# The MLP's second multiplication: three of eight weight units in seven block products, groups of 1024 columns over all PSUM banks

## The chip, the cores and the metric

The kernel runs on one core of a Trainium2 chip (trn2). Its time is the device time of one execution in microseconds (us). The kernel before takes 1953.93 us, the median of 3 runs (1953.6 to 1954.25). TensorE (PE in the profile) multiplies, VectorE (DVE) and ScalarE (ACT) prepare operands and take results away, GpSimd (POOL) does small work, and SyncE (SP) issues most of the DMAs.

## The reference

One decoder layer on 256 tokens of width 2048: a combined attention and retention layer, a cross attention, and an MLP. The change touches only the MLP and the norm at its end:

```python
D_FF = 4 * D_MODEL                                   # 8192
nm = rmsnorm(h, mlp_norm_w)
h = h + jnp.square(jax.nn.relu(nm @ w_up)) @ w_down  # (256, 2048) @ (2048, 8192), then (256, 8192) @ (8192, 2048)
...
return rmsnorm(h, final_norm_w)
```

All arrays are float32, and so is the result.

## The kernel before

TensorE multiplies in a one-pass format that holds fewer bits than float32. So each operand is split into a high part `hi` and a rest `lo` (`split`, L161 to L163): ScalarE copies the source into `hi` (L162), then VectorE computes `lo` = source - `hi` (L163), one instruction each for 128 partitions by 1024 elements. A product then takes three matmuls: hi by hi, hi by lo, lo by hi (`mul`, L158).

Weights come as a stream. `chunk` (L189) takes one of three `raw` buffers of 1 MB, issues one DMA for it on SP's queue (L195), and splits it into two pairs of `hi` and `lo` tiles; there are four buffers of each. A `raw` buffer is free for the next DMA when VectorE has read it last, and a `hi` or `lo` buffer when TensorE has.

The MLP (`mlp`) works in two halves of 4096 hidden columns. In the first part of a half, called *up* here, eight `wgroup` calls multiply by `w_up`, with the weights as TensorE's stationary operand and matmuls of 256 columns. After each group `up_evac` takes the PSUM result through ReLU on ScalarE (L1052), a product on VectorE (L1053) and a split into `hh` and `hl`, which hold hidden columns on the partitions. In the second part, *down*, four `xgroup` calls multiply by 512 columns of `w_down` each, over 4096 rows. There the hidden tiles are stationary and the weights move through, 512 columns per matmul, for two tiles of 128 tokens (i = 0 and 1). `down_evac` adds the PSUM result, times `r2`, to the residual `hres` (L1066). In the last half it also takes the squares (L1073), the product with the final gain (L1076) and, at the very end, the scale by the final norm and the output DMAs (L1090, L1091).

The order of the instructions on each engine is made when the kernel is built, by a scheduler that goes by the dependencies and its own costs; the engine then runs its list in that order. PSUM has eight banks of 512 float32 per partition: two tiles of two banks (`mm`), three of one (`ps`), one of one (`po`). SBUF tiles of 1024 float32 (`big`) come from a pool of 30.

Of the kernel before, what the change touches and what calls it, by code (L numbers as in the profile page):

```python
# [17 lines left out]
P = 128  # L18
# [47 lines left out]
class Kern:  # L66
# [104 lines left out]
    def rsqrt(self, out, v, s):  # L171
# [213 lines left out]
    def retention(self):  # L385
# [242 lines left out]
    def keys(self):  # L628
# [255 lines left out]
    def merge(self):  # L884
# [58 lines left out]
    def cross(self):  # L943
# [70 lines left out]
        for h in range(2):  # L1014
# [8 lines left out]
                                        rows=512) for j in range(4)]))  # L1023

    def mlp(self):
        nc, a = self.nc, self.a
        V, A, G, PE = nc.vector, nc.scalar, nc.gpsimd, nc.tensor
        hres = [None] * 4
        s8, r2 = self.keep("hs8", [2, 4]), self.keep("r2", [2])

        # the residual with tokens on the partitions, and its mean square
        def back(j, i):
            if i == 0:
                hres[j] = self.big("hres", F32, (2, 512))
# [3 lines left out]
            V.tensor_copy(hres[j][:, i, :], pt)  # L1038
# [9 lines left out]

        def up_evac(hh, hl):
# [9 lines left out]
        f8, ft = self.keep("fs", [2, 4]), self.keep("ft", [2])  # L1059
        fw, outs = [], []  # L1060

        # hidden = relu(u)^2 with u not yet divided by the rms: 1 / (mean square) at the end
        def down_evac(f, j):
            def evac(i, ps):
                o = hres[j][:, i, :]
                V.scalar_tensor_tensor(o, ps, r2[:, i:i + 1], o, op0=ALU.mult, op1=ALU.add)  # L1066
                if f == 0:
                    return
                if not fw:
                    fw.append(self.raw())  # L1070
                    nc.sync.dma_start(fw[0], a["final_norm_w"].partition_broadcast(P))
                junk = self.w2("junk")
                A.activation(junk, o, AF.Square, accum_out=f8[:, i, j:j + 1])  # L1073
                if i == 0:
                    outs.append(self.big("out", F32, (2, 512)))
                V.tensor_tensor(outs[j][:, i, :], o, fw[0][:, j * 512:(j + 1) * 512], op=ALU.mult)  # L1076
                v = ft[:, i:i + 1]
                if j == 2:
                    V.tensor_reduce(v, f8[:, i, 0:3], axis=AX.X, op=ALU.add)
                    V.tensor_scalar(v, v, 1.0 / D, EPS, op0=ALU.mult, op1=ALU.add)  # L1080
                if j < 3:
# [47 lines left out]
```

## Time and profile before

| | |
|---|---|
| median of 3 runs | 1953.93 us |
| the profiled execution: span of its instructions | 1951.9 us |
| the runs' median less this span | 2.0 us |
| TensorE busy | 1933.5 us (99%) |
| VectorE busy | 1145.7 us (59%) |
| ScalarE busy | 937.3 us (48%) |

The page gives the span, from the first to the last instruction; what lies around it, some 2 us, is in the time of a run and not in the span. The busy share of TensorE is of pipelined matmuls, whose records overlap, so the pace is read from their starts. The MLP takes the span from about 1238 us on: up, down, up, down, with the borders at 1402.7, 1569 and 1764.8 us.

### The profile page before, as it was taken

How to read it: one execution, taken by the hardware profiler on the slowest of the kernel's cores; microseconds unless marked ns; L12 is line 12 of the kernel's file. 1: busy time of each engine (PE TensorE's matmuls, PEld its weight loads, DVE VectorE, ACT ScalarE, POOL GpSimd, SP SyncE). 2: the span in 40 equal slices, each digit the busy share in tenths (PEclk: the TensorE clock that was granted, in tenths of full speed). 3: DMA queues.
4: the chain of work that ended last, by engine and by line, in shares of the span. 5: the costliest groups of instructions: out<-in, count | busy, mean ns of one | idle time of the engine just before them, and what ended most of it. 6: DMA issues, size and time to landing. Idle time of an engine off the chain costs nothing.

```text
span 1951.9 us, 28137 instructions
## 1 busy us (share of the span) xinstructions
PE 1933.5 (99%) x11606; PEld 1714.9 (88%) x11606; DVE 1145.7 (59%) x1327; ACT 937.3 (48%) x1214; POOL 85.3 (4%) x101
## 2 busy tenths in 40 slices
PE   8999999999999999999999999999999999999998
PEld 6888889888899999888889999999988899998886
DVE  6554577555756666886556756555544445554454
ACT  6444444454555555766445545544433344444442
POOL 1100021000000000321000000000000000000000
PEclk9999999999999999999999999999999999999999
DMA  7555544677876775434566654565655555655554
GB/s 269 210 174 192 186 172 175 229 249 245 274 248 244 248 254 176 137 112 140 184 208 232 208 173 154 172 191 177 193 184 184 193 189 179 189 178 194 188 179 151
DMA packets 190017, 382.29 MB, mean 196 GB/s; under 512 B 10576, under 2 KB 18768, under 8 KB 189760
## 3 DMA queue, kind: packets, MB, share of 16 engines
q1 hardware_dynamic: 185872, 375.01, 57.2%
q10 hardware_dynamic: 3216, 3.15, 0.5%
q0 software_dynamic: 800, 2.33, 0.4%
q8 instruction: 91, 1.49, 0.3%
q14 instruction: 38, 0.31, 0.0%
HBM read 374.17 MB, written 6.29 MB: 195 GB/s over the span
## 4 chain that ended last, share of the span: by engine, by line
PE 97%; DVE 1%; ACT 0%; issue 0%; DMA 0%; POOLq 0%; POOL 0%; DVEq 0%
PE x L158 52%; PE w L158 36%; PE acc L158 3%; PE o L158 1%; PE s L158 1%; PE ro L158 1%; PE pT L816 1%; DMA anw<-in_attn_norm_w_dram 0%; DVE lo L163 0%; PE tr L287 0%; PE rs L158 0%; ACT hi L162 0%; DVE bl L163 0%; PE xo L158 0%; PE g L158 0%
## 5 line engine op out<-in xcount | busy, mean ns | idle before, releaser
L163 DVE TENSOR_TENSOR lo<-raw,hi 128x1024 fp32r<-128x1024 f32 x688 | 848.6, 1240 | 702.8 <-ACT hi L162 688.1
L162 ACT ACTIVATE hi<-raw 128x1024 fp32r<-128x1024 f32 x688 | 724.1, 1059 | 913.2 <-PE x L158 526.0
L158 PE MATMUL w<-nh,hi 128*128 128x256 f32 x1088 | 308.2, 283 | 0.0
L158 PE MATMUL w<-nh,lo 128*128 128x256 f32 x1088 | 307.5, 283 | 0.0
L158 PE MATMUL w<-nl,hi 128*128 128x256 f32 x1088 | 306.9, 282 | 0.0
L158 PE MATMUL x<-hi,xh 128*128 128x512 f32 x704 | 282.5, 401 | 2.2 <-ACT hi L162 2.2
L158 PE MATMUL x<-hi,xl 128*128 128x512 f32 x704 | 278.0, 395 | 0.0
L158 PE MATMUL x<-lo,xh 128*128 128x512 f32 x704 | 277.2, 394 | 0.0
L158 PEld LDWEIGHTS w<-nl,hi 128*128 128x128 f32 x1088 | 207.1, 190 | 0.0
L158 PEld LDWEIGHTS w<-nh,hi 128*128 128x128 f32 x1088 | 207.1, 190 | 0.0
L158 PEld LDWEIGHTS w<-nh,lo 128*128 128x128 f32 x1088 | 206.8, 190 | 0.0
L158 PE MATMUL x<-hi,hl 128*128 128x512 f32 x512 | 202.7, 396 | 0.0
L158 PE MATMUL x<-hi,hh 128*128 128x512 f32 x512 | 202.3, 395 | 0.0
L158 PE MATMUL x<-lo,hh 128*128 128x512 f32 x512 | 201.0, 393 | 0.0
L158 PEld LDWEIGHTS x<-lo,xh 128*128 128x128 f32 x704 | 133.1, 189 | 30.9 <-DVE lo L163 0.8
L158 PEld LDWEIGHTS x<-hi,xh 128*128 128x128 f32 x704 | 132.8, 189 | 30.1 <-ACT hi L162 2.6
L158 PEld LDWEIGHTS x<-hi,xl 128*128 128x128 f32 x704 | 132.8, 189 | 26.5
L158 PE MATMUL w<-xh,hi 128*128 128x256 f32 x512 | 145.3, 284 | 0.0
L158 PE MATMUL w<-xh,lo 128*128 128x256 f32 x512 | 144.2, 282 | 0.0
L158 PE MATMUL w<-xl,hi 128*128 128x256 f32 x512 | 144.1, 281 | 0.0
L158 PEld LDWEIGHTS x<-lo,hh 128*128 128x128 f32 x512 | 96.6, 189 | 22.7
L158 PEld LDWEIGHTS x<-hi,hh 128*128 128x128 f32 x512 | 96.2, 188 | 23.1
(257 smaller groups left out, 2572.9 us busy)
## 6 DMA issues: line engine op xcount, KB each, us to landing
raw<-in_w_in_dram SPq DMA_DIRECT2D x119, 1024.0 KB, 4.9
raw<-in_w_up_dram SPq DMA_DIRECT2D x64, 1024.0 KB, 5.3
raw<-in_w_down_dram SPq DMA_DIRECT2D x64, 1024.0 KB, 5.1
raw<-in_cmp_w_k_dram SPq DMA_DIRECT2D x16, 1024.0 KB, 4.9
raw<-in_w_b_dram SPq DMA_DIRECT2D x16, 1024.0 KB, 5.2
raw<-in_cmp_w_v_dram SPq DMA_DIRECT2D x16, 1024.0 KB, 5.0
raw<-in_w_a_dram SPq DMA_DIRECT2D x16, 1024.0 KB, 5.1
raw<-in_w_out_dram SPq DMA_DIRECT2D x16, 1024.0 KB, 5.1
```

The lines of the kernel that those rows point to most:

```text
L158: self.pin(self.nc.tensor.matmul(out, l, r, start=start, stop=stop, skip_group_check=True))
L162: self.pin(self.nc.scalar.activation(hi, src, AF.Copy))
L163: self.pin(self.nc.vector.tensor_tensor(lo, src, hi.bitcast(F32), op=ALU.subtract))
L816: PE.transpose(pt[:, r * P:(r + 1) * P], sms[r // 2][:, r % 2, c:c + P], self.ident)
```

## The change

The down part is computed in *units* of 256 rows by 1024 columns of `w_down`: a 2 by 2 grid of blocks, each 128 rows by 512 columns, against a 2 by 2 grid of hidden blocks (two row tiles by two token tiles). A plain unit (P) does the eight block products as before, 24 matmuls. A unit of kind S does seven (Strassen's scheme, in Winograd's form), 21 matmuls, with sums of blocks as operands. The kinds of the eight units of a group are "SPPSPSPP".

- The hidden columns now go in four passes (p = 0 to 3) of 2048 in place of two halves of 4096: four `wgroup` calls, then two groups (c = 0 and 1) of 1024 output columns over the eight units of the pass.
- For each S unit, `up_evac` also makes four sums of hidden blocks (`unit_sums`: four VectorE instructions of 128x128, one split of 512).
- For each S unit, `seven` makes four combinations of weight blocks on VectorE (`f1` of 1024, two of 512 into `f2`), and splits them and the four plain blocks: splits of 512, 1024, 1024 and 1024, where a plain unit has two of 1024.
- A group holds all eight PSUM banks: four for results that go straight to the output (`xa`, `xb`), four for the products m1, m5, m6, m7. These four are summed after the last S unit (`down_combine`).
- At the end, the product with the final gain is done in place in `hres`, in tiles of 1024.

```diff
+    def unit_sums(self, y, u, wide):
...
+        s1, s2, s3, s4 = (s[:, k * P:(k + 1) * P] for k in range(4))
+        V.tensor_tensor(s1, a21, a22, op=ALU.add)
+        V.tensor_tensor(s2, s1, a11, op=ALU.subtract)
+        V.tensor_tensor(s3, a21, a11, op=ALU.subtract)
+        V.tensor_tensor(s4, a12, s2, op=ALU.subtract)
+        self.split(sh, sl, s)
...
+    def ugroup(self, w, r0, c0, kinds, ah, al, sums, combine, evac, tail=1):
...
+        ab, cd = self.mmt("xa"), self.mmt("xb")
+        bank[2], bank[3] = ab[:, :512], ab[:, 512:]
+        bank[4], bank[8] = cd[:, :512], cd[:, 512:]
...
+        def plain(us):
...
+                    self.split(h, l, raw[:, k * 1024:(k + 1) * 1024])
...
+            for i in range(2):
+                for j in range(2):
+                    for u in us:
+                        for k in range(2):
+                            product((2, 3, 4, 8)[2 * i + j], act(u, k, i), B[u, k, j], u == n - 1 and k == 1)
+                if us[-1] == n - 1:
+                    evac(i, (ab, cd)[i])
+                yield
+
+        def seven(u):
+            raw = load(u)
+            q = raw.rearrange("p (q n) -> p q n", q=4)
+            f1, f2 = self.big("t1", F32, (2, 512)), self.big("t2", F32, (2, 512))
+            V.tensor_tensor(f1, q[:, 1:2, :].to_broadcast([P, 2, 512]), q[:, 0::3, :], op=ALU.subtract)
+            V.tensor_tensor(f2[:, 0, :], q[:, 3, :], f1[:, 0, :], op=ALU.subtract)
+            V.tensor_tensor(f2[:, 1, :], q[:, 2, :], f2[:, 0, :], op=ALU.subtract)
+            dh, dl = hilo()
+            self.split(dh[:, :512], dl[:, :512], q[:, 0, :])
+            (h1, t1), (h2, t2) = [[self.big(n, F32R, (2, 512)) for n in ("th", "tl")] for _ in range(2)]
+            self.split(h1, t1, f1)
+            self.split(h2, t2, f2)
+            bh, bl = hilo()
+            self.split(bh, bl, raw[:, 1024:])
...
+            for k, m in enumerate((1, 5, 7, 6, 4, 2, 3)):
+                product(m, x[m], b[m], u == last_s and m in (1, 5, 6, 7))
...
     def mlp(self):
...
+        KINDS = "SPPSPSPP"
+        NP = 4
...
+        def down_combine(c):
+            def combine(bank):
...
+                A.activation(x[:, :512], bank[1], AF.Copy)
+                V.tensor_tensor(u2, bank[6], x[:, :512], op=ALU.add)
+                V.tensor_tensor(y[:, :512], bank[7], u2, op=ALU.add)
+                V.tensor_tensor(x[:, 512:], bank[5], u2, op=ALU.add)
+                V.tensor_tensor(y[:, 512:], bank[5], y[:, :512], op=ALU.add)
+                for i, t in enumerate((x, y)):
+                    o = hres[i, c]
+                    V.scalar_tensor_tensor(o, t, r2[:, i:i + 1], o, op0=ALU.mult, op1=ALU.add)
...
-        for f in range(2):
-            hh, hl = [], []
-            self.run(self.seq(*[self.wgroup(a["w_up"][0], f * 4096 + 512 * j, self.h2h, self.h2l, up_evac(hh, hl))
-                                for j in range(8)]))
-            self.run(self.seq(*[self.xgroup(a["w_down"][0], 512 * j, hh, hl, down_evac(f, j), r0=f * 4096, rows=4096,
-                                            last=(f == 1 and j == 3)) for j in range(4)]))
+        for p in range(NP):
+            hh, hl, sums = [], [], {}
+            self.run(self.seq(*[self.wgroup(a["w_up"][0], p * 2048 + 512 * j, self.h2h, self.h2l,
+                                            up_evac(hh, hl, sums)) for j in range(4)]))
+            self.run(self.seq(*[self.ugroup(a["w_down"][0], p * 2048, 1024 * c, KINDS, hh, hl, sums,
+                                            down_combine(c), down_evac(p, c), tail=2 if (p, c) == (NP - 1, 1) else 1)
+                                for c in range(2)]))
```

Below, U0 to U7 are the units of the first group (c = 0) of a pass and V0 to V7 those of the second; U0, U3, U5, V0, V3 and V5 are of kind S.

First place: VectorE's list where up ends and down begins. Before, around the product with ReLU of the last up group (L1053):

```order
L163 TENSOR_TENSOR lo_12830<-raw_12827,hi_12829 128x1024
L163 TENSOR_TENSOR lo_12834<-raw_12827,hi_12833 128x1024
L1053 TENSOR_TENSOR relu_12785<-relu_12785,w_12552 128x1024
L163 TENSOR_TENSOR lo_12864<-raw_12861,hi_12863 128x1024
L163 TENSOR_TENSOR hl_12789<-relu_12785,hh_12788 128x1024
L163 TENSOR_TENSOR lo_12868<-raw_12861,hi_12867 128x1024
L163 TENSOR_TENSOR lo_12898<-raw_12895,hi_12897 128x1024
```

Behind that product stand one weight split, the split of the hidden tile (`hl`) and more weight splits. Now, at the same place of pass p = 0 (raw_11860 is U0, raw_11908 U1, raw_11942 U2, raw_11976 U3; L1103 is `f1`, L1104 and L1105 the two halves of `f2`, `tl` the rests of their splits):

```order
L163 TENSOR_TENSOR lo_11915<-raw_11908,hi_11914 128x1024
L1169 TENSOR_TENSOR relu_11851<-relu_11851,w_11618 128x1024
L163 TENSOR_TENSOR lo_11945<-raw_11942,hi_11944 128x1024
L163 TENSOR_TENSOR hl_11855<-relu_11851,hh_11854 128x1024
L1103 TENSOR_TENSOR t_1823_11862<-raw_11860 128x1024
L1104 TENSOR_TENSOR t_1824_11863<-raw_11860,t_1823_11862 128x512
L1105 TENSOR_TENSOR t_1824_11863<-raw_11860,t_1824_11863 128x512
L163 TENSOR_TENSOR tl_11872<-t_1823_11862,th_11871 128x1024
L163 TENSOR_TENSOR tl_11874<-t_1824_11863,th_11873 128x1024
L1103 TENSOR_TENSOR t_1848_11978<-raw_11976 128x1024
L1104 TENSOR_TENSOR t_1849_11979<-raw_11976,t_1848_11978 128x512
L1105 TENSOR_TENSOR t_1849_11979<-raw_11976,t_1849_11979 128x512
```

The combinations of U0 stand behind the product with ReLU (now L1169) and behind `hl`; those of U3 follow, ahead of the second split of U2. The four passes have the same order here.

Second place: TensorE's list at the same border. Before, the last two matmuls of up and the first of down (`hi_12795` and `lo_12796` are the weights, `hh` and `hl` the hidden tiles):

```order
L158 MATMUL w_12552<-nl_10788,hi_12733 128x256
L158 MATMUL w_12552<-nh_10787,lo_12734 128x256
L158 MATMUL x_12792<-hi_12795,hh_11071 128x512
L158 MATMUL x_12792<-hi_12795,hl_11072 128x512
L158 MATMUL x_12792<-lo_12796,hh_11071 128x512
L158 MATMUL x_12792<-hi_12795,hh_11071 128x512
```

Now, in pass p = 0, where m_1833, m_1836, m_1835 and m_1834 are the banks of m1, m5, m7 and m6:

```order
L158 MATMUL w_11618<-nh_10787,lo_11800 128x256
L158 MATMUL m_1833_11883<-hi_11867,hh_11071 128x512
L158 MATMUL m_1833_11883<-hi_11867,hl_11072 128x512
L158 MATMUL m_1833_11883<-lo_11868,hh_11071 128x512
L158 MATMUL m_1836_11886<-th_11871,sh_11076 128x512
L158 MATMUL m_1836_11886<-th_11871,sl_11077 128x512
L158 MATMUL m_1835_11885<-th_11871,sh_11076 128x512
L158 MATMUL m_1836_11886<-tl_11872,sh_11076 128x512
L158 MATMUL m_1835_11885<-th_11871,sl_11077 128x512
L158 MATMUL m_1835_11885<-tl_11872,sh_11076 128x512
L158 MATMUL m_1834_11884<-th_11873,sh_11076 128x512
```

Three matmuls of U0 (m1) follow the up part; from the fourth on TensorE's list needs `th_11871`, the high part of `f1`.

Third place: VectorE's list in the last down part. Before, where its second column group has ended (the evacuations of L1066, then the products with the gain):

```order
L163 TENSOR_TENSOR lo_16416<-raw_16413,hi_16415 128x1024
L1066 SCALAR_TENSOR_TENSOR hres_10993<-x_16096,r_10798,hres_10993 128x512 x2
L1076 TENSOR_TENSOR out_16372<-hres_10993,raw_16086 128x512 x2
L163 TENSOR_TENSOR lo_16420<-raw_16413,hi_16419 128x1024
L163 TENSOR_TENSOR lo_16450<-raw_16447,hi_16449 128x1024
```

Now, in pass p = 3 between its groups c = 0 and c = 1 (raw_17070 is V0, raw_17118 V1, raw_17152 V2; `xa` and `xb` are c = 0's results):

```order
L1200 SCALAR_TENSOR_TENSOR hres_10894<-xa_16736,r_10798,hres_10894 128x1024
L1209 TENSOR_TENSOR hres_10894<-hres_10894,fw_17043 128x1024
L1212 TENSOR_SCALAR ft<-fs 128x1
L1200 SCALAR_TENSOR_TENSOR hres_10949<-xb_16737,r_10798,hres_10949 128x1024
L163 TENSOR_TENSOR lo_17121<-raw_17118,hi_17120 128x1024
L1103 TENSOR_TENSOR t_2608_17072<-raw_17070 128x1024
L1209 TENSOR_TENSOR hres_10949<-hres_10949,fw_17043 128x1024
L1212 TENSOR_SCALAR ft<-fs 128x1
L1104 TENSOR_TENSOR t_2609_17073<-raw_17070,t_2608_17072 128x512
L163 TENSOR_TENSOR lo_17125<-raw_17118,hi_17124 128x1024
L1105 TENSOR_TENSOR t_2609_17073<-raw_17070,t_2609_17073 128x512
L163 TENSOR_TENSOR tl_17082<-t_2608_17072,th_17081 128x1024
```

The combinations of V0 stand behind both evacuations of c = 0 here; in the passes p = 0 to 2 `f1` of the second group's first unit stands ahead of them.

## Rows read from the trace of the kernel before

**Rows 1.** The page, engines: busy us (share), instructions.
```profile
PE 1933.5 (99%) x11606; PEld 1714.9 (88%) x11606; DVE 1145.7 (59%) x1327; ACT 937.3 (48%) x1214; POOL 85.3 (4%) x101
```
**Rows 2.** The page, chain that ended last: shares of the span.
```profile
PE 97%; DVE 1%; ACT 0%; issue 0%; DMA 0%; POOLq 0%; POOL 0%; DVEq 0%
```
**Rows 3.** The chain in order of time, MLP: start us, us, work, count.
```profile
1402.86 178.38 PE x L158 x768
1581.24 183.60 PE w L158 x1536
```
**Rows 4.** Windows, first up and down: us, busy of PE, PEld, DVE, ACT, POOL, PEclk, DMA.
```profile
1238.00:1402.00 164.00, 164.00 (x1377) 164.00 (x1376) 88.96 (x79) 75.66 (x81) 0.00 (x0) 1.00 0.57 182
1403.00:1569.00 166.00, 166.00 (x716) 134.41 (x715) 79.21 (x68) 65.28 (x62) 0.00 (x0) 1.00 0.56 187
```
**Rows 5.** Timeline, TensorE, first matmul of down: start us, us, instruction.
```profile
1402.69 0.40 PE L158 MATMUL x<-hi,hh 128*128 128x512 f32 x1
```
**Rows 6.** Timeline, ScalarE, same border: in brackets, idle before and releaser.
```profile
1402.78 1.06 ACT L162 ACTIVATE hi<-raw 128x1024 fp32r<-128x1024 f32 x1 [1.82 <-PE w L158]
1403.74 1.01 ACT L1052 ACTIVATE relu<-w 128x1024 f32<-128x1024 f32 x1
1405.47 1.06 ACT L162 ACTIVATE hi<-raw 128x1024 fp32r<-128x1024 f32 x1 [0.72 <-PE x L158]
1406.44 1.04 ACT L162 ACTIVATE hh<-relu 128x1024 fp32r<-128x1024 f32 x1
```
**Rows 7.** Timeline, VectorE, same border.
```profile
1403.87 1.23 DVE L163 TENSOR_TENSOR lo<-raw,hi 128x1024 fp32r<-128x1024 f32 x1 [1.66 <-ACT hi L162]
1405.01 1.21 DVE L1053 TENSOR_TENSOR relu<-relu,w 128x1024 f32<-128x1024 f32 x1
1406.57 1.23 DVE L163 TENSOR_TENSOR lo<-raw,hi 128x1024 fp32r<-128x1024 f32 x1 [0.34 <-ACT hi L162]
1407.71 1.22 DVE L163 TENSOR_TENSOR hl<-relu,hh 128x1024 fp32r<-128x1024 f32 x1
```
**Rows 8.** Groups by line and shape, VectorE, then ScalarE: busy us, mean ns, idle.
```profile
L163 DVE TENSOR_TENSOR pl<-pT,ph 128x512 fp32r<-128x512 f32 x24 | 16.4, 682 | 0.4
...
L1066 DVE SCALAR_TENSOR_TENSOR hres<-x,r,hres 128x512 f32<-128x512 f32 x16 | 11.4, 747 | 10.3 <-PE x L158 10.3
...
L163 DVE TENSOR_TENSOR kcat<-ky,kcat 128x128 fp32r<-128x128 f32 x16 | 3.4, 284 | 0.0
...
L162 ACT ACTIVATE blk<-blkf 128x512 fp32r<-128x512 f32 x8 | 4.9, 628 | 3.2 <-DVE blkf L582 3.2
```
**Rows 9.** Tile raw in the first down part: from a DMA's issue to its landing.
```profile
DMA to landing us min/median/max: 4.9/5.1/5.5
```
**Rows 10.** Timeline, TensorE, the kernel's first matmuls.
```profile
12.27 0.63 PE L158 MATMUL x<-hi,xh 128*128 128x512 f32 x1
12.70 0.63 PE L158 MATMUL x<-hi,xl 128*128 128x512 f32 x1
...
15.47 0.39 PE L158 MATMUL x<-hi,xl 128*128 128x512 f32 x1
15.70 0.39 PE L158 MATMUL x<-lo,xh 128*128 128x512 f32 x1
```
**Rows 11.** Windows behind the last matmul.
```profile
1945.00:1947.00 2.00, 0.00 (x0) 0.00 (x0) 1.30 (x4) 0.72 (x2) 0.55 (x1) 1.00 0.00 0
1947.00:1948.00 1.00, 0.00 (x0) 0.00 (x0) 0.14 (x1) 0.00 (x0) 0.00 (x0) 0.58 0.80 299
1948.00:1949.00 1.00, 0.00 (x0) 0.00 (x0) 0.00 (x0) 0.00 (x0) 0.00 (x0) 0.50 1.01 377
```
**Rows 12.** Timeline, VectorE, the end.
```profile
1943.49 0.75 DVE L1066 SCALAR_TENSOR_TENSOR hres<-x,r,hres 128x512 f32<-128x512 f32 x1 [1.95 <-PE x L158]
...
1945.86 1.28 DVE L1090 TENSOR_SCALAR out<-out,ft 128x512 f32<-128x512 f32 x3 [0.67 <-POOL ft L1084]
```

More of the change, by code (lines that the diff above doesn't have):

```diff
@@ L1023, in cross @@
                                         rows=512) for j in range(4)]))
+    def unit_sums(self, y, u, wide):
+        V = self.nc.vector
+        v = y[:, 2 * u:2 * u + 2, :].rearrange("p k (i t) -> p k i t", i=2)
+        a11, a21, a12, a22 = v[:, 0, 0, :], v[:, 0, 1, :], v[:, 1, 0, :], v[:, 1, 1, :]
+        s = self.w2("ss")
+        if wide:
+            both = self.big("sb", F32R, (2, 512))
+            sh, sl = both[:, 0, :], both[:, 1, :]
+        else:
+            sh, sl = self.w2("sh", 512, F32R), self.w2("sl", 512, F32R)
+        s1, s2, s3, s4 = (s[:, k * P:(k + 1) * P] for k in range(4))
[4 more added lines that the diff above has]
+        self.split(sh, sl, s)
+        return [(sh[:, k * P:(k + 1) * P], sl[:, k * P:(k + 1) * P]) for k in range(4)]
@@ new lines, in ugroup, with product, act, load @@
+    def ugroup(self, w, r0, c0, kinds, ah, al, sums, combine, evac, tail=1):
+        A, V = self.nc.scalar, self.nc.vector
+        n = len(kinds)
+        last_s = max(u for u in range(n) if kinds[u] == "S")
+        bank = {}
+        ab, cd = self.mmt("xa"), self.mmt("xb")
+        bank[2], bank[3] = ab[:, :512], ab[:, 512:]
+        bank[4], bank[8] = cd[:, :512], cd[:, 512:]
+        started = set()
+        def product(m, x, b, last):
+            (xh, xl), (bh, bl) = x, b
+            o = bank[m]
+            self.mul(o, xh, bh, m not in started, False)
+            self.mul(o, xl, bh, False, False)
+            self.mul(o, xh, bl, False, last)
+            started.add(m)
+        def act(u, k, i):
+            kt = 2 * u + k
+            s = slice(i * P, (i + 1) * P)
+            return ah[kt // 4][:, kt % 4, s], al[kt // 4][:, kt % 4, s]
+        def load(u):
+            raw = self.raw()
+            src = w[r0 + u * 256:r0 + (u + 1) * 256, c0:c0 + 1024].rearrange("(k p) n -> p k n", p=P)
+            self.nc.sync.dma_start(raw.rearrange("p (k n) -> p k n", k=2), src)
+            return raw
+        def hilo():
+            return (self.st.tile([P, 1024], F32R, name=self.nm("hi"), tag="hi"),
+                    self.st.tile([P, 1024], F32R, name=self.nm("lo"), tag="lo"))
+        def plain(us):
+            B = {}
+            for u in us:
+                raw = load(u)
+                for k in range(2):
+                    h, l = hilo()
+                    self.split(h, l, raw[:, k * 1024:(k + 1) * 1024])
+                    for j in range(2):
+                        s = slice(j * 512, (j + 1) * 512)
+                        B[u, k, j] = h[:, s], l[:, s]
+            for i in range(2):
+                for j in range(2):
+                    for u in us:
+                        for k in range(2):
+                            product((2, 3, 4, 8)[2 * i + j], act(u, k, i), B[u, k, j], u == n - 1 and k == 1)
[3 more added lines that the diff above has]
+        def seven(u):
+            raw = load(u)
+            q = raw.rearrange("p (q n) -> p q n", q=4)
[10 more added lines that the diff above has]
+            self.split(bh, bl, raw[:, 1024:])
+            b = {1: (dh[:, :512], dl[:, :512]), 2: (bh[:, :512], bl[:, :512]), 3: (bh[:, 512:], bl[:, 512:]),
+                 5: (h1[:, 0, :], t1[:, 0, :]), 7: (h1[:, 1, :], t1[:, 1, :]),
+                 6: (h2[:, 0, :], t2[:, 0, :]), 4: (h2[:, 1, :], t2[:, 1, :])}
+            s1, s2, s3, s4 = sums[u]
+            x = {1: act(u, 0, 0), 2: act(u, 1, 0), 3: s4, 4: act(u, 1, 1), 5: s1, 6: s2, 7: s3}
+            if 1 not in bank:
+                bank[1], bank[6], bank[7], bank[5] = self.pst("m1"), self.pst("m6"), self.pst("m7"), self.pot("m5")
+            for k, m in enumerate((1, 5, 7, 6, 4, 2, 3)):
+                product(m, x[m], b[m], u == last_s and m in (1, 5, 6, 7))
+                if k == 3:
+                    if u == last_s:
+                        combine(bank)
+                    yield
+            yield
+        u = 0
+        while u < n:
+            if kinds[u] == "S":
+                yield from seven(u)
+                u += 1
+            else:
+                us = list(range(u, n)) if n - u == tail else [u]
+                yield from plain(us)
+                u += len(us)
@@ L1037, in back @@
                 PE.transpose(pt[:, b * P:(b + 1) * P], self.h2[j][:, b, i * P:(i + 1) * P], self.ident)
-            V.tensor_copy(hres[j][:, i, :], pt)
+            V.tensor_copy(o, pt)
             junk = self.w2("junk")
@@ L1047, in mlp, with up_evac @@
             self.after(6 + 3 * n, lambda n=n: back(n // 2, n % 2))
-        def up_evac(hh, hl):
+        def up_evac(hh, hl, sums):
             def evac(ps):
@@ L1056, in evac @@
                 self.split(hh[-1], hl[-1], y)
-            return evac
-        f8, ft = self.keep("fs", [2, 4]), self.keep("ft", [2])
-        fw, outs = [], []
-        def down_evac(f, j):
+                for u in range(2):
+                    k = 2 * len(hh) - 2 + u
+                    if KINDS[k] == "S":
+                        sums[k] = self.unit_sums(y, u, len(sums) == 2)
+            return evac
+        def down_combine(c):
+            def combine(bank):
+                u2 = self.w2("u2")
+                x, y = self.big("ux", F32, (1024,)), self.big("uy", F32, (1024,))
+                A.activation(x[:, :512], bank[1], AF.Copy)
[6 more added lines that the diff above has]
+                    V.scalar_tensor_tensor(o, t, r2[:, i:i + 1], o, op0=ALU.mult, op1=ALU.add)
+            return combine
@@ L1064, in evac, with down_evac @@
+        f8, ft = self.keep("fs", [2, 2]), self.keep("ft", [2])
+        fw = []
+        def down_evac(p, c):
             def evac(i, ps):
-                o = hres[j][:, i, :]
+                o = hres[i, c]
                 V.scalar_tensor_tensor(o, ps, r2[:, i:i + 1], o, op0=ALU.mult, op1=ALU.add)
-                if f == 0:
+                if p < NP - 1:
                     return
                 if not fw:
-                    fw.append(self.raw())
-                    nc.sync.dma_start(fw[0], a["final_norm_w"].partition_broadcast(P))
@@ L1072, in evac @@
[L1072 to L1076, printed above, removed]
+                    for k in range(2):
+                        fw.append(self.big("fw", F32, (1024,)))
+                        nc.scalar.dma_start(fw[k], a["final_norm_w"][k * 1024:(k + 1) * 1024].partition_broadcast(P))
@@ L1077, in evac @@
+                junk = self.big("junk", F32, (1024,))
+                A.activation(junk, o, AF.Square, accum_out=f8[:, i, c:c + 1])
+                V.tensor_tensor(o, o, fw[c], op=ALU.mult)
                 v = ft[:, i:i + 1]
[L1078 to L1081, printed above, removed]
+                if c == 0:
+                    V.tensor_scalar(v, f8[:, i, 0:1], 1.0 / D, EPS, op0=ALU.mult, op1=ALU.add)
```

11 lines of the change are left out of this document (6 added, 5 removed).

## The prediction

> **What bounds the kernel now.** I read four views in this order. The page's engine line has TensorE busy for 99% of the span and VectorE for 59% [rows 1]; as matmul records overlap, that alone proves little. The chain of waits settles it: 97% of the span is TensorE [rows 2], and in order of time the MLP is unbroken runs of matmuls [rows 3]. They also give the pace: 178.38 us for 768 matmuls of 512 columns is 0.232 us each. The windows show what lies beside: in up, VectorE is busy 88.96 of 164 us, in down 79.21 of 166, at a granted clock of 1.00 [rows 4]. So what leaves TensorE's list shortens the run, as long as VectorE and ScalarE, which have half their time free, hand over operands in time. The fourth view, the timelines at the border from up to down [rows 5 to 7], shows how late VectorE is there with work that needs up's last result.
>
> **What goes.** Before, a group of 512 columns over 4096 rows takes 192 matmuls; the same work now is half as many rows by twice the columns, with 5 x 24 + 3 x 21 = 183. There are 8 groups: 72 matmuls fewer, 72 x 0.232 = 16.7 us, all on the path if nothing waits.
>
> **What comes, on VectorE.** A plain unit costs it two splits of 1.23 us [rows 7], 2.5 us, in 24 x 0.232 = 5.6 us of TensorE. An S unit costs `f1` (1024 elements, taken as 1.23), two halves of `f2` and a split of 512 (0.68 each [rows 8]), and three splits of 1.23: 7.0 us, in 4.9 us of TensorE. A group adds the combine, four of 512 at 0.7 and two of 1024 at 1.28 (L1066's 0.747 for 512 [rows 8] plus 1.23 - 0.68 for the other half), and two evacuations at 1.28: 7.9 us. That sums to 5 x 2.5 + 3 x 7.0 + 7.9 = 41.4 us in 183 x 0.232 = 42.5 us of TensorE. So VectorE, half idle before, has almost no slack left in a group, and it gains little ahead, since `hi` and `lo` are two units deep and `raw` three. `unit_sums` adds 4 x 0.28 + 0.68 = 1.8 us three times a pass [rows 8], in the half-empty up part: nothing on the path.
>
> **The border from up to down, four times.** This is the term that decides. I count in us from the first matmul of down, 1402.69 [rows 5]. Up's last result goes through ScalarE's ReLU (ends at 2.1 [rows 6]) and VectorE's product (ends at 3.5); `hh` ends at 4.8; `hl` starts at 5.0 and ends at 6.2 [rows 6, 7]. Before, nobody needs these soon. Now VectorE's list has U0's `f1` behind `hl` (first order listing of the change), so on the same rows `f1` runs from 6.2 to 7.4 and the halves of `f2` to 8.1 and 8.8. ScalarE takes `th` of `f1` some 0.2 later (as `hh` follows its product [rows 6, 7]), 7.6 to 8.7. VectorE's `tl` ends at 10.0; `th` of `f2` at 10.1; its `tl` at 11.3. TensorE has three matmuls (m1, 0.7 us), and its fourth needs `th` of `f1`. It stands from 0.7 to 8.7, then runs three, three from 10.0, two from 10.7, and the twelfth at 11.3. Nine are left: U0 ends at 11.3 + 10 x 0.232 = 13.6, where 21 x 0.232 = 4.9 was due. That is 8.7 us at full clock.
>
> What the clock does on top: behind the kernel's last matmul, which began at 1943.07, the granted clock is 1.00 up to 1947, 0.58 in the next us, then 0.50, the lower level, 1.2 GHz [rows 11]. A stand of 8.0 us is longer than that. At the lower level 512 columns take 0.43 us, as in the first matmuls at 12.27 and 12.70, and 0.23 is back by 15.47, 5 us after the first of them began [rows 10]. So from 8.7 to 13.5 or so matmuls go at 0.43: three from 8.7, three from 10.0, eight more by 13.5 and a bit, the other seven at 0.232; U0 ends near 15.1, a delay of 10.2. The Trainium skill has the rule (TensorE: Matmul & The Clock Gate, section "Part 1: The HAM clock gate"): the throttled clock is the default, sustained activity releases it, and idle time takes it back. By that rule each border costs the 10.2; without it the 8.7 stands. Both ends come from rows; I take 10.2, since rows 11 show the fall for a shorter stand.
>
> After it, U3's `raw` is the buffer that `f2` frees at 8.8; its DMA lands 5.1 us later [rows 9], at 13.9. U3's combinations and rests stand ahead of U2's second split in VectorE's list, which so ends near 20.2. TensorE needs it at 20.4 at full clock, later at the lower. That split frees U5's `raw`, which lands at 25.3; `f1`, `f2` and one `tl` of U5, then U4's two splits, end at 31.5. TensorE wants the last at 30.9 at full clock (0.6 us more, 9.3 in all) and at 32.2 after the slower start (nothing more). By landings 1.5 us later it would be some 2 us more. Lower bound for the border: `hl` and `f1` lie one behind the other whatever the rest does, which with a faster hand-over is 8 us. Range 8 to 12, value 10.2, four times: 40.8.
>
> **The other joints.** From c = 0 to c = 1 in passes 0 to 2, the evacuation of `xb` and the last `tl` of V0 end within 0.3 us of TensorE's need by the same count: 0 to 1.5 each, taken as 0.3, together 1. In pass 3 VectorE's list has both evacuations and a product with the gain, which waits for the square of the same tile, ahead of `f1` (third listing). From TensorE's first matmul of c = 1: product to 1.5, second evacuation to 3.0, a split to 4.1, `f1` to 5.3, `th` ready at 6.6, `f2` at 9.0, the last `tl`, behind a gain product and two splits, at 12.6. TensorE does four matmuls at 6.6, nine from 10.3, the rest from 12.6: V0 ends at 13.8 instead of 4.9, 8.9 late, and up to 10.7 at the lower clock; taken as 9.8. From down to up nothing is added: both PSUM tiles are freed by the evacuations, and the first weight splits are done ahead. At the end the evacuation is 0.5 longer (1.28 for 0.75 [rows 12]), the square 0.4 (ScalarE's 1.06 for 0.63 [rows 6, 8]), and the product with the gain now waits for that square and delays the scale by 1.3: 2.3 us.
>
> **Sum.** -16.7 + 40.8 + 1 + 9.8 + 2.3 = +37.2 us. The profiled span of 1951.9 becomes 1989.1; with the 2.0 us around it, 1991.1 beside the median of 1953.9.
>
> **Rivals.** (1) The borders are hidden: `f1`, `f2` and their splits of U0 are ready before up's last result. Then 1953.9 - 16.7 + 2.3 = 1939.5, faster. For it speaks VectorE's free time in up [rows 4]; against it the order, in which a list waits at its head: they would have to stand ahead of the product with ReLU, and in no pass they do. 4%. (2) Half hidden, near no change: a border would have to cost 14.4 / 4 = 3.6 us or less, while `th` alone is 8 us late. 3%. (3) The stand costs no clock: 4 x 9.3 + 8.9 + 1 + 2.3 - 16.7 = +32.7, 1986.6. For it: the matmuls between 8.7 and 11.3 wait for VectorE anyway; against: rows 11. 15%. (4) VectorE becomes the bound of whole groups: with 41.4 of 42.5 us filled, waits for landings and for ScalarE inside an S unit can't be caught up, and each of the eight groups ends some 5 us later: +40 more, 2031. For it: VectorE waits 3 us for a landing twice in c = 0 by the count above; against: the count finds c = 1, whose first landing is early, on time. It decides as soon as a group loses over 1 us of VectorE beside its work. 10%. The forecast has 68%.
>
> **How the numbers follow.** 1991 is the likeliest. Low end: 4 x 8 + 8 + 1 - 17 = +24, and some for waits that are shorter than counted: 1975. High end: 4 x 12 + 4.5 + 10.7 + 2.5 - 16.7 = +49, and part of rival 4: 2010. A measurement of this kernel can tell 0.2%, 3.9 us, from no change; of the cases only rival 1 is faster by more, rival 2 is within it: faster 4%, same 3%, slower 93%.
>
> **What would show it.** Between each up and down, TensorE idle about 8 us, released by ScalarE's `th` of `f1`, with 0.43 us matmuls and a granted clock near 0.5 behind it; a similar stand inside the last down part; 72 matmuls fewer; VectorE near 95% busy in the groups. The forecast is wrong if TensorE runs through the borders (rivals 1, 2), if the clock stays at 1.00 there (3), or if VectorE is waited for in every S unit (4).

## The result, and the profile after

The changed kernel takes 1988.9 us, the median of 4 runs (1988.14 to 1989.28), beside 1953.8 (1953.6 to 1954.25) for the kernel before on the same chip: a ratio of 1.0179, with a 95% interval of 1.0167 to 1.0192 (the numbers in brackets behind the ratios below are such intervals). It is slower by 35.1 us; the forecast was 1991. The profiled execution took 1988.6 us, with a span of 1986.8.

The page of the changed kernel, engines and the chain's shares, beside [rows 1, 2]:

```profile
PE 1928.8 (97%) x11534; PEld 1708.4 (86%) x11534; DVE 1305.6 (66%) x1549; ACT 979.1 (49%) x1274; POOL 85.3 (4%) x101
PE 94%; DVE 3%; ACT 1%; DMA 1%; issue 1%; POOLq 0%; POOL 0%; DVEq 0%; SPq 0%; ACTq 0%
```

TensorE has the 72 instructions fewer, yet its busy time falls by 4.7 us only, since some of the rest ran at the lower clock. The list of TensorE's waits (us in total, times, longest) has one line in the MLP that the kernel before has not:

```profile
PE m L158 <- ACT th L162: 35.6, 6, 7.3
```

Six waits for `th`, the high part of `f1` or `f2`. Four of them are the borders from up to down. TensorE's timeline at the first (start, us, instruction; idle before and releaser in brackets), where before it ran on [rows 5]:

```profile
1310.92 0.40 PE L158 MATMUL m<-hi,hh 128*128 128x512 f32 x1
1311.15 0.40 PE L158 MATMUL m<-hi,hl 128*128 128x512 f32 x1
1311.39 0.40 PE L158 MATMUL m<-lo,hh 128*128 128x512 f32 x1
1319.07 0.79 PE L158 MATMUL m<-th,sh 128*128 128x512 f32 x1 [7.29 <-ACT th L162]
1319.66 0.63 PE L158 MATMUL m<-th,sl 128*128 128x512 f32 x1
...
1324.15 0.56 PE L158 MATMUL xb<-tl,hh 128*128 128x512 f32 x1
1324.55 0.40 PE L158 MATMUL xa<-hi,hh 128*128 128x512 f32 x1
```

VectorE there, beside [rows 7] (L1169 is the product with ReLU, L1103 `f1`, L1104 and L1105 the halves of `f2`):

```profile
1313.23 1.22 DVE L1169 TENSOR_TENSOR relu<-relu,w 128x1024 f32<-128x1024 f32 x1
...
1315.57 1.23 DVE L163 TENSOR_TENSOR hl<-relu,hh 128x1024 fp32r<-128x1024 f32 x1
1316.71 1.22 DVE L1103 TENSOR_TENSOR t<-raw 128x1024 f32<-128x1024 f32 x1
1317.96 0.69 DVE L1104 TENSOR_TENSOR t<-raw,t 128x512 f32<-128x512 f32 x1
1318.69 0.69 DVE L1105 TENSOR_TENSOR t<-raw,t 128x512 f32<-128x512 f32 x1
```

and ScalarE, beside [rows 6] (its first line is the split of U0's first block, the only 512 wide split of a weight there):

```profile
1302.41 0.63 ACT L162 ACTIVATE hi<-raw 128x512 fp32r<-128x512 f32 x1 [1.80 <-PE w L158]
...
1317.96 1.06 ACT L162 ACTIVATE th<-t 128x1024 fp32r<-128x1024 f32 x1 [2.43 <-DVE t L1103]
```

Read them upwards: the matmul at 1319.07 waits for `th`, which begins as `f1` ends; `f1` has all its data, since ScalarE had read U0's `raw` at 1302.41, 14 us earlier; it stands behind `hl`, which stands behind the product with ReLU, and VectorE has no idle time between them. Windows around it (us; busy of PE, PEld, DVE, ACT, POOL; granted clock, DMA share, GB/s):

```profile
1311.60:1319.00 7.40, 0.19 (x1) 0.00 (x0) 6.84 (x7) 4.41 (x5) 0.00 (x0) 0.68 0.42 142
1319.00:1324.50 5.50, 5.43 (x12) 4.00 (x13) 5.43 (x7) 2.22 (x4) 0.00 (x0) 0.50 0.56 191
1324.50:1406.00 81.50, 81.50 (x353) 66.15 (x352) 65.68 (x66) 37.92 (x41) 0.00 (x0) 1.00 0.57 186
```

The clock falls during the stand, the twelve matmuls behind it run at the lower level (0.50, 1.2 GHz), and from 1324.5 on TensorE never stands while VectorE is 81% busy. The other two waits are the joint between the groups of the last pass:

```profile
1923.58 0.40 PE L158 MATMUL m<-lo,hh 128*128 128x512 f32 x1
1928.92 0.79 PE L158 MATMUL m<-th,sh 128*128 128x512 f32 x1 [4.95 <-ACT th L162]
...
1932.46 0.79 PE L158 MATMUL m<-th,sh 128*128 128x512 f32 x1 [1.46 <-ACT th L162]
```

Behind the last matmul, which begins at 1974.69, come 12.1 us, 8.8 before. VectorE's timeline there (L1200 evacuation, L1209 product with the gain, L1208 the square on ScalarE), beside [rows 12]:

```profile
1974.60 1.23 DVE L1209 TENSOR_TENSOR hres<-hres,fw 128x1024 f32<-128x1024 f32 x1 [1.22 <-ACT junk L1208]
...
1975.81 1.28 DVE L1200 SCALAR_TENSOR_TENSOR hres<-xb,r,hres 128x1024 f32<-128x1024 f32 x1
...
1978.88 1.22 DVE L1209 TENSOR_TENSOR hres<-hres,fw 128x1024 f32<-128x1024 f32 x1 [0.61 <-ACT junk L1208]
```

The table below carries most readings of the experiments. It gives the length of each down part, from its first matmul to the first of the next up (p3 only to the start of its last matmul, which leaves out that matmul's 0.2), read from starts in the timelines; "ideal" is the number of matmuls by 0.2323 (178.38 / 768 [rows 3]). "End" is the time from the start of the last matmul to the end of the span, 8.8 us in the kernel before.

| kernel | ideal | p0 | p1 | p2 | p3 | end | time, us |
|---|---|---|---|---|---|---|---|
| the change | 85.0 | 95.03 | 95.26 | 93.67 | 104.28 | 12.1 | 1988.9 |
| e1_plain | 89.2 | 89.44 | 88.74 | 88.60 | 88.78 | 11.3 | 1955.45 |
| e2_s135 | 85.0 | 85.60 | 85.46 | 85.68 | 87.12 | 12.3 | 1945.05 |
| e3_s246 | 85.0 | 85.05 | 85.09 | 84.82 | 84.62 | 13.4 | 1941.66 |
| e4_fill | 85.0 | 93.03 | 92.67 | 92.93 | 103.45 | 12.1 | 1982.39 |
| e5_hoist | 85.0 | 84.88 | 84.84 | 84.77 | 94.96 | 12.4 | 1949.81 |
| e6_c0 | 85.7 | 85.59 | 85.17 | 84.99 | 95.19 | 12.3 | 1952.08 |
| e7_4s | 83.6 | 88.33 | 88.34 | 86.78 | 88.15 | 13.4 | 1953.29 |
| e8_end | 85.0 | 85.08 | 85.12 | 84.87 | 84.71 | 12.2 | 1940.28 |
| e9_mix (p3: 85.0) | 84.3 | 84.28 | 84.30 | 84.10 | 84.92 | 12.2 | 1938.44 |
| e10_out | 85.0 | 95.21 | 93.80 | 94.46 | 104.19 | 11.2 | 1988.65 |

### The profile page after: what moved, and what is told of

Its sections match the earlier page's. It is cut to its first block, busy times and chain, and to the rows that moved or that the text cites. A ratio compares the mean times of both kernels' runs of the same rounds, so it can differ in the third digit from the quotient of the medians.

```text
span 1986.8 us, 28293 instructions
## 1 busy us (share of the span) xinstructions
PE 1928.8 (97%) x11534; PEld 1708.4 (86%) x11534; DVE 1305.6 (66%) x1549; ACT 979.1 (49%) x1274; POOL 85.3 (4%) x101
## 4 chain that ended last, share of the span: by engine, by line
PE 94%; DVE 3%; ACT 1%; DMA 1%; issue 1%; POOLq 0%; POOL 0%; DVEq 0%; SPq 0%; ACTq 0%
PE w L158 36%; PE x L158 33%; PE xa L158 7%; PE xb L158 6%; PE m L158 4%; PE acc L158 3%; DVE lo L163 1%; PE o L158 1%; PE s L158 1%; PE ro L158 1%; PE pT L816 1%; ACT hi L162 0%; DMA anw<-in_attn_norm_w_dram 0%; DVE t L1103 0%; DMA rep<-in_c_rep_dram 0%
## 5 line engine op out<-in xcount | busy, mean ns | idle before, releaser
L163 DVE TENSOR_TENSOR lo<-raw,hi 128x1024 fp32r<-128x1024 f32 (+1 forms) x688 | 833.0, 1221 | 569.6 <-ACT hi L162 545.5
L162 ACT ACTIVATE hi<-raw 128x1024 fp32r<-128x1024 f32 (+1 forms) x688 | 709.6, 1043 | 848.4 <-PE x L158 336.7
L158 PEld LDWEIGHTS w<-xh,hi 128*128 128x128 f32 x512 | 96.8, 189 | 1.4
L158 PEld LDWEIGHTS w<-xl,hi 128*128 128x128 f32 x512 | 96.8, 189 | 1.4
L158 PEld LDWEIGHTS w<-xh,lo 128*128 128x128 f32 x512 | 96.8, 189 | 0.0
L158 PE MATMUL w<-mh,hi 128*128 128x256 f32 x320 | 90.6, 283 | 0.0
L158 PE MATMUL w<-ml,hi 128*128 128x256 f32 x320 | 90.0, 281 | 0.0
```

Of the source, the lines that this page charges most:

```text
L158: self.pin(self.nc.tensor.matmul(out, l, r, start=start, stop=stop, skip_group_check=True))
```

## The experiments

The theory is that of the forecast: the loss comes from the first unit of a pass being of kind S, whose sums stand in VectorE's list behind up's last result. The main rival was that seven products overload VectorE in whole groups.

**e1_plain: no unit by seven products.**

```diff
-        last_s = max(u for u in range(n) if kinds[u] == "S")
+        last_s = max((u for u in range(n) if kinds[u] == "S"), default=-1)
...
-        KINDS = "SPPSPSPP"
+        KINDS = "PPPPPPPP"
```

> All eight units of a group are plain (no seven-product units, no sums, no combine); four passes, groups of 1024 columns over the banks xa and xb and the end stay as in the change. Theory (the stands of TensorE come from VectorE's work for the S unit that opens a group, behind up's last result): no stand of more than 1 us in the MLP, the matmul count of before, so the time of before plus the longer end: 1953.8 + 2.3 = 1956. Rival (four passes and groups of 1024 columns over all banks cost the time by themselves, by more borders and by evacuations in larger pieces): 1965 to 1975, with idle of TensorE at the borders or where a group ends.

1955.45 us, ratio 1.0006 (0.9996 to 1.0015). No new wait. Four passes, groups of 1024 columns and all PSUM banks cost nothing that can be told in the time (the end alone is 2.5 us longer in the profile); so the 35 us hang on the S units.

**e2_s135 and e3_s246: the same three S units a group, one place or two places later.**

```diff
-        KINDS = "SPPSPSPP"
+        KINDS = "PSPSPSPP"      # e2
+        KINDS = "PPSPSPSP"      # e3
```

> The S units stand at places 1, 3 and 5 of a group instead of 0, 3 and 5: one plain unit, 5.6 us of TensorE, lies ahead of the first. VectorE's work in sum is the same. Theory: a border's stand shrinks by about that cover, from 8 us to 2 to 4 us, too short for the lower clock, and the joint in pass 3 shrinks as well: 1988.9 - 4 x 7 - 6 = about 1955 (1948 to 1962). Rival (VectorE, with 41.4 of 42.5 us filled, is the bound of every group): the place doesn't matter, 1983 to 1990.

> The S units stand at places 2, 4 and 6: two plain units, 11.2 us of TensorE, lie ahead of the first. Theory: no stand of over 1 us at the borders, clock at 1.00, the 16.7 us of the 72 matmuls are kept but for the longer end: 1953.8 - 16.7 + 2.3 = 1939.5, up to 1946 if VectorE's little slack costs 1 us a group. Rival (VectorE is the bound of every group): 1975 or more, TensorE waiting in every S unit.

e2: 1945.05, ratio 0.9953 (0.9938 to 0.9968). e3: 1941.66, ratio 0.9936 (0.992 to 0.9953). The page of e3:

```profile
PE 1916.7 (99%) x11534; PEld 1700.7 (88%) x11534; DVE 1300.6 (67%) x1549; ACT 978.2 (50%) x1274; POOL 86.3 (4%) x101
```

These are the instruction counts of the change, on TensorE and on VectorE, and 47 us less; e3's down parts are at TensorE's ideal. Its time lies 2.2 above the 1939.5 of its theory, as its end is 4.6 us longer than before and not 2.3: both products with the gain stand ahead of the scale in VectorE's list there. VectorE was never full, as a window over its first down part shows:

```profile
1311.30:1396.30 85.00, 85.00 (x368) 68.69 (x367) 77.08 (x83) 45.02 (x49) 0.00 (x0) 1.00 0.59 191
```

That ends the rival of an overloaded VectorE for three S units. With S at the second place I had expected a stand: the plain unit's 24 matmuls are too short to cover `th`. That was a miss: e2 has next to no stand (0.8 us of waits for `th` in all) and is 10 us faster than the 1955 expected. Its TensorE timeline shows why:

```profile
1313.67 0.40 PE L158 MATMUL m<-hi,hh 128*128 128x512 f32 x1
...
1314.60 0.40 PE L158 MATMUL xb<-hi,hh 128*128 128x512 f32 x1
...
1317.88 0.40 PE L158 MATMUL xa<-hi,sh 128*128 128x512 f32 x1
...
1321.14 0.40 PE L158 MATMUL m<-th,sh 128*128 128x512 f32 x1
```

Between the first product of the S unit (1313.67) and its first matmul with `th` (1321.14) the scheduler had put matmuls of other units (the `xb` results of the plain unit first) and those of the S unit itself that need no `th`. At the head of a pass in the change, TensorE's list holds such matmuls too, but behind those with `th`: U0's products m2 and m3 run from 1324.55 on, though VectorE had ended their weight split at 1307.6. So the order of TensorE's list may have a part in the stand as well; no run here moves that alone.

**e4_fill: the stand filled.** 30 more matmuls, whose results are overwritten, behind the first product of U0 in the first group of each pass.

```diff
             for k, m in enumerate((1, 5, 7, 6, 4, 2, 3)):
                 product(m, x[m], b[m], u == last_s and m in (1, 5, 6, 7))
+                if k == 0 and u == 0 and c0 == 0:
+                    for _ in range(30):
+                        self.mul(bank[5], x[1][0], b[1][0], True, False)
```

> The change, with 30 more matmuls of 512 columns behind m1 of the first unit after each border, into the bank of m5, which the first matmul of m5 clears; they fill 7.0 of the 7.7 us of each stand and add nothing to what is computed. Theory (half speed after the stand costs 1.5 us a border on top of the stand): granted clock 1.00 through the four borders, 4 x 1.5 = 5 to 6 us less than the change, 1983. Rival (after the stand TensorE waits for VectorE anyway, so its clock costs nothing): 1988.9, the same. Rival (the fill delays operands or runs over): slower than 1989.

1982.39 us, ratio 1.0144 (1.0128 to 1.0159): 6.5 less than the change, with more work. TensorE there:

```profile
1312.20 7.13 PE L158 MATMUL m<-hi,hh 128*128 128x512 f32 x30
1319.65 0.50 PE L158 MATMUL m<-th,sh 128*128 128x512 f32 x1 [0.32 <-ACT th L162]
1319.99 0.39 PE L158 MATMUL m<-th,sl 128*128 128x512 f32 x1
```

The first matmul with `th` comes no earlier (8.2 us after down's first in both), but what follows runs at 0.23, and the granted clock is 1.00 through all four borders. By the table the borders of passes 0 to 2 lose 2.0, 2.6 and 0.7 us less. In pass 3 the border loses 8.0 for 10.2 (TensorE's time up to the joint, less 186 matmuls and the fill), but the joint 1.4 more: behind it the lower clock lasts 5.8 us for 3.0. So the clock's share of a border is 1.9 us on average, and the rest, some 7.9, is the late `th`. One reserve: behind the fill the scheduler also put matmuls of the next units between those with `th` and `tl`, so a part of this may be the order.

**e5_hoist: U0's load and sums moved ahead.** The load of U0, its `f1` and `f2` and their splits are issued in the last group of up, and so stand earlier in VectorE's list; the work is the same.

```diff
+            self.after(AT, lambda p=p, pre=pre: pre.append(self.combos(a["w_down"][0], p * 2048, 0)))
...
-            raw = load(u)
+            if u == 0 and pre:
+                raw, h1, t1, h2, t2 = pre[0]
+                q = raw.rearrange("p (q n) -> p q n", q=4)
+                dh, dl = hilo()
+                self.split(dh[:, :512], dl[:, :512], q[:, 0, :])
...
```

> The change as it is (units 0, 3 and 5 by seven products), and one thing moved: for the first 1024 columns the load of unit 0, its sums f1 and f2 and their splits stand in the last group of the up part, ahead of the product with ReLU in VectorE's list. Nothing is taken away or added. Theory (the stands come from the place of U0's sums in VectorE's list behind the product with ReLU): the four waits of 7.3 us on th and the half-level stretches behind them go, the joint inside the last pass stays (about 10 us); 1988.9 less four times 10 = 1948, range 1944 to 1953. Rival (seven products at the head of a group cost VectorE or the weight queue this work wherever it stands): TensorE waits in the up part instead, or for the second unit's weights, and the time stays at 1965 or above.

1949.81 us, ratio 0.9978 (0.9969 to 0.9987), 39.1 less than the change. VectorE's timeline (here L1055 and L1056 are U0's `f2`, L1191 the product with ReLU), then TensorE's:

```profile
1298.00 0.68 DVE L1056 TENSOR_TENSOR t<-raw,t 128x512 f32<-128x512 f32 x1
...
1300.87 1.21 DVE L163 TENSOR_TENSOR tl<-t,th 128x1024 fp32r<-128x1024 f32 x1
...
1313.14 1.21 DVE L1191 TENSOR_TENSOR relu<-relu,w 128x1024 f32<-128x1024 f32 x1
```

```profile
1311.30 0.40 PE L158 MATMUL m<-lo,hh 128*128 128x512 f32 x1
1311.53 0.39 PE L158 MATMUL m<-th,sh 128*128 128x512 f32 x1
```

The sums and their splits are done at 1302.1, over 9 us before TensorE asks for them, up is not longer for it, and all four borders are gone with the same S units and the same work. In the change U0's data had landed well before `f1` (above), so it is the place in the list that counts, not the load. The joint of the last pass stays: 94.96 + 0.2 - 85.0 = 10.2 us.

**e6_c0: the first unit of a pass plain, and so two S units in the first group.** The second group keeps three.

```diff
-            self.run(self.seq(*[self.ugroup(a["w_down"][0], p * 2048, 1024 * c, KINDS, hh, hl, sums,
+            self.run(self.seq(*[self.ugroup(a["w_down"][0], p * 2048, 1024 * c, ("PPPSPSPP", KINDS)[c], hh, hl, sums,
```

> Only the first 1024 columns of each pass get another order of units, plain ones at 0, 1, 2, 4, 6, 7 (seven products at 3 and 5); the second 1024 columns keep 0, 3 and 5. That gives back 3 of the 72 matmuls in each pass, 12 in all, or 2.8 us. Theory: the four border stands go with about 40 us, the joint between the two halves of the last pass stays, alone, with waits of 5 to 7 us on th and 8 to 10 in all: 1988.9 - 40 + 2.8 = 1951.7, range 1948 to 1955. Rival (the order of units at the head matters in both halves): the joints of passes 0 to 2 open too, and it is 1960 or above.

1952.08 us, ratio 0.9991 (0.9982 to 1.0). The one wait left is that of the last joint:

```profile
PE m L158 <- ACT th L162: 6.4, 2, 4.9
```

p0 to p2 are at their ideal, though V0 is still an S unit: the joints of passes 0 to 2 cost nothing, and that of pass 3 costs 95.19 + 0.2 - 85.7 = 9.7 us.

**e7_4s: where VectorE does become the bound.** Four S units a group.

```diff
-        KINDS = "SPPSPSPP"
+        KINDS = "PPSSPSSP"
...
-                        sums[k] = self.unit_sums(y, u, len(sums) == 2)
+                        sums[k] = self.unit_sums(y, u, len(sums) >= 2)
```

> Four units of eight by seven products (2, 3, 5 and 6), plain ones at the borders: 24 matmuls fewer than with three, 5.6 us of TensorE. VectorE's sums of a whole group rise to 4 plain units of 2.5 us, 4 of 7.0 and 7.9 of evacuation, 45.9 us, against 180 matmuls of 0.232, 41.8. Theory that VectorE is the bound once its sum passes TensorE's (my rival of the prediction, one unit further on): up to 4 us lost in each of 8 groups, less 5.6: 1960 to 1970 against the 1941.7 of units 2, 4 and 6. Rival (durations of VectorE are counted too high, or ScalarE's share hides them): no waits, 1941.7 - 5.6 = 1936.

1953.29 us, ratio 0.9997 (0.9988 to 1.0006). Neither number, though the first theory's mechanism. TensorE's waits, its timeline at the first joint between c = 0 and c = 1, and a window from the border to there:

```profile
PE xa L158 <- DVE hres L1200: 11.8, 4, 3.0
```

```profile
1352.83 0.39 PE L158 MATMUL xb<-lo,hh 128*128 128x512 f32 x1
1356.19 0.50 PE L158 MATMUL xa<-hi,hh 128*128 128x512 f32 x1 [2.98 <-DVE hres L1200]
...
1358.41 0.63 PE L158 MATMUL xa<-hi,hh 128*128 128x512 f32 x1
1358.83 0.63 PE L158 MATMUL xa<-hi,hl 128*128 128x512 f32 x1
```

```profile
1316.00:1356.20 40.20, 37.22 (x162) 29.88 (x160) 40.12 (x44) 23.61 (x26) 0.00 (x0) 1.00 0.59 203
```

VectorE is busy all the time (40.12 of 40.20 us), ends the group late, the evacuation frees the bank late, and a part loses (88.33 + 88.34 + 86.78 + 88.15 - 4 x 83.6) / 4 = 4.3 us. That is a wait of 2.9 to 3.0 and, in three of the four, some 1.6 of lower clock behind it. It lies near the 45.9 - 41.8 = 4.1 of the count by luck: the wait alone is less, as the records of VectorE overlap (`hl` and `f1` above start 1.14 us apart and last 1.23 and 1.22) and a sum of durations is too high. And it is paid in four groups, not eight: behind c = 1 comes up, and no wait shows there. 4 x 4.3 - 5.6 = +11.6, as measured against e3.

**e9_mix: four S units only where up follows.** On top of e8 below, in passes 0 to 2.

```diff
-        KINDS = "PPSPSPSP"
+        KINDS = ("PPSSPSPP", "PPSSPSSP")      # c = 0, c = 1
+        LAST = ("PPSPSPSP", "PPSPSPSP")
...
```

> From the run at 1940.28: in passes 0 to 2 the second 1024 columns get four units by seven products (2, 3, 5 and 6), the first ones 2, 3 and 5; the last pass keeps 2, 4 and 6. That is 9 matmuls fewer, 2.1 us of TensorE. Theory (VectorE's backlog of a group with four such units, some 4 us, costs only where another group of the same kind follows; the up part behind the second columns takes it up, since one of its banks is free and VectorE has slack in it): 1940.3 - 2.1 = 1938.2, range 1937.5 to 1939.2. Rival (the backlog delays the first evacuation of up, or units 2 and 3 side by side in the first columns leave a wait at the joint): 1 us or more lost in each of three passes, 1941 or above.

1938.44 us, ratio 0.992 (0.9907 to 0.9934): no wait in the MLP, all parts at their ideal. It is the fastest of all, 15.6 us under the kernel before.

**e8_end and e10_out: the product with the gain out of place,** in e3 and in the change.

```diff
-                V.tensor_tensor(o, o, fw[c], op=ALU.mult)
+                outs[i, c] = self.big("out", F32, (1024,))
+                V.tensor_tensor(outs[i, c], o, fw[c], op=ALU.mult)
...
-                    o = hres[i, k // 2][:, (k % 2) * 512:(k % 2) * 512 + 512]
+                    o = outs[i, k // 2][:, (k % 2) * 512:(k % 2) * 512 + 512]
```

> Units 2, 4 and 6 as in the run at 1941.7, and the product with the last norm's weights writes a tile of its own instead of over its input, so that it has not to wait for ScalarE's square of the same tile. Theory (the end is long since a whole group of 1024 columns ends at once, and its product waits on the square: 0.61 and 1.22 us in the list): 1.2 less, 1940.4, range 1939.8 to 1941.2. Rival (the square of the second half, the sum of squares and the scaling follow one another whatever the product does): no change, 1941.7.

> The change as it is, and only the product with the last norm's weights writes a tile of its own. Theory: the wait of that product on ScalarE's square stands in VectorE's list twice, ahead of the sums of unit 0 at the joint of the last pass (1.22 us) and at the end (0.61); without it 1.2 to 1.5 go at the end, as in the run at 1940.28, and 0.6 to 1.2 at the joint: 1988.9 - 2.3 = 1986.6, range 1985.8 to 1987.6; the longest wait on th there falls from 4.95 to some 4. Rival (the joint is set by the loads or by the work itself): only the end gets shorter, 1987.6, and the wait stays at 4.95.

e8: 1940.28 us, ratio 0.9931 (0.9918 to 0.9943), 1.4 less than e3 as expected; in the profiles the end takes 12.2 us for 13.4. e10: 1988.65 (1986.81 to 1988.97), 0.3 less than the change and inside the spread of either: a miss. In its profile the end is 0.9 shorter (11.2 us behind the start of the last matmul, for 12.1), but the last part is not (104.19 for 104.28). VectorE there, first in the change, then in e10 (where L1210 is the product):

```profile
1923.03 1.23 DVE L1209 TENSOR_TENSOR hres<-hres,fw 128x1024 f32<-128x1024 f32 x1 [1.22 <-ACT junk L1208]
...
1926.56 1.22 DVE L1103 TENSOR_TENSOR t<-raw 128x1024 f32<-128x1024 f32 x1
1927.69 1.22 DVE L1209 TENSOR_TENSOR hres<-hres,fw 128x1024 f32<-128x1024 f32 x1
```

```profile
1919.86 1.23 DVE L1210 TENSOR_TENSOR out<-hres,fw 128x1024 f32<-128x1024 f32 x1
...
1923.65 1.22 DVE L1210 TENSOR_TENSOR out<-hres,fw 128x1024 f32<-128x1024 f32 x1
...
1924.86 1.21 DVE L1103 TENSOR_TENSOR t<-raw 128x1024 f32<-128x1024 f32 x1
```

The wait on the square is gone, but the scheduler now puts the second product ahead of `f1` (L1103), where it stood behind it: 1.2 us won, 1.2 given back. The longest wait at this joint is 5.23 us, not the 4 expected, for 4.95 in the change; and as the border ahead of it lost 9.0 us for 10.2, the joint itself took 10.4 for 9.3.

## Why the prediction was right, step by step

- **What goes.** 72 matmuls; e3 has no wait in the MLP and its parts are at the ideal, so 0.232 each held.
- **The border.** The mechanism is the one forecast, and e5 shows it with the same work. Counted from down's first matmul, `f1` ran from 5.8 to 7.0 and `th` was there at 8.1, where I had 6.2 to 7.4 and 8.7: VectorE's split ahead of `hl` began earlier than in the kernel before, and `th` followed `f1` at once, not 0.2 later. U0's follow-up cost nothing, as counted, though for another reason: U3's `f1` ran at 1321.65 without waiting for its load, which I had put behind `f2` of U0 and landing at 1324.8. That load was issued at 1313.34, as VectorE's last split of U1 ended.
- **The clock.** Its share was taken as 1.5 a border (10.2 less 8.7); e4 gives 1.9 on average, with its reserve. Two steps of that count are loose. It names 3 + 3 + 8 + 7 = 21 matmuls behind the stand where 18 are left; the end at 15.1 comes out with 11 at 0.43 and 7 at 0.232. And the 5 us to the full pace run from the first matmul of 512 columns, at 10.42, which [rows 10] do not show; from the 12.27 shown they are 3.2. The granted clock reads 1.00 from 12 to 13 us, so those rows do not show the level; the border of the change does (0.43 from start to start at 0.50).

```profile
10.42 0.80 PE L158 MATMUL x<-hi,xh 128*128 128x512 f32 x1 [2.22 <-ACT hi L162]
```

- **Sizes.** The borders lose 10.0, 10.3 and 8.7 us in p0 to p2 and 10.2 in p3 (TensorE reaches the joint 53.4 us after that part's start at 1870.41, for 186 x 0.2323 = 43.2): 39.2, forecast 40.8. The joints of passes 0 to 2 cost nothing (e6), forecast 1. p3 loses 19.5 with its last matmul, so the last joint takes 9.3, forecast 9.8 (10.2 in e5, 9.7 in e6). The end takes 3.3 for 2.3; I had missed that the first half's product, held by its own square, stands ahead of the last evacuation (1974.60 to 1975.8). Together -16.7 + 39.2 + 9.3 + 3.3 = +35.1, and the spans differ by 34.9; forecast +37.2. That the total came within 2.1 is in part luck: borders and joints were 3.1 too high, the end 1.0 too low.
- **VectorE's load.** One sign did not come: VectorE near 95% busy in the groups. It was 81% busy in the change (65.68 of 81.50 above) and 91% in e3 (77.08 of 85.00), where TensorE never stands. The 41.4 of 42.5 us summed durations whose records overlap, and so left VectorE too little slack.
- **Rivals.** (1) and (2) are out by the stands. (3), no cost of the clock, gives 1986.6, as near the result as the forecast; it is the windows and e4 that refute it, not the time: with the clock held at the borders the measured time is 1982.4, since the late `th` costs 7.9 a border and not 9.3. (4) is out by e3; e7 shows the mechanism one S unit further on, though not its price, and that a group's overrun is paid only where another such group follows.

On the rule that I weighed (the Trainium skill, TensorE: Matmul & The Clock Gate, "Part 1: The HAM clock gate": idle time takes the full clock back, activity restores it), this trace agrees at the borders: 0.68 as the mean over the stand, 0.50 behind it, 1.00 from 1324.5 on, 5.4 us after the stand's end.

## What to carry to other kernels

Saving matmuls in a kernel that TensorE bounds pays in full only if the operands' new preparation is early enough at the seams, where one stage ends and the next begins: ask of each first unit of a stage what stands ahead of its sums in VectorE's list, and put units with long preparation behind plain ones. Here the order of the same eight units decided between 35 us lost and 12 won. Compare each engine's busy time in a stage with TensorE's, read from a trace, since a sum of durations is too high where records overlap: with VectorE 91% busy (e3) only the seams mattered; where it was busy without a break (e7) TensorE waited, but only where the stage behind had no room for the overrun (not behind e7's second groups, nor in e9).

## What was not expected of the hardware

- Waits of 2.9 to 3.0 us were enough for the lower clock in three of e7's four joints: matmuls start every 0.43 us behind the one of 2.98 (1358.41 and 1358.83 above). Behind the third joint's wait of 2.93 none did, and that part is 1.6 us shorter (86.78 for 88.33). Ahead of e2 I had called stands of 2 to 4 us too short for it.
- The return of the full clock varies between equal stands. At the third border of the change 0.23 us was back 3.7 us after the first matmul, not 5.5, and that part is 1.4 us shorter (93.67 for 95.03); in e10_out it was the second border (93.80) and the fourth.

```profile
1693.06 0.80 PE L158 MATMUL m<-th,sh 128*128 128x512 f32 x1 [7.29 <-ACT th L162]
...
1696.72 0.40 PE L158 MATMUL m<-tl,sh 128*128 128x512 f32 x1
1696.95 0.39 PE L158 MATMUL xb<-th,hh 128*128 128x512 f32 x1
```
